# A two-layer decoder trunk on one core: the second half of the residual moved ahead of the second F-chunk's gate products, and the Strassen products of two places moved back by one chunk

## The chip, the cores and the metric

The kernel runs on one core of a Trainium2 chip. The metric is the device time of one execution in microseconds (us); below it is the median of three runs. One more execution was profiled; its trace has, for every instruction, the engine, the line of the kernel, the tiles, the start and the duration. Engines: PE multiplies matrices, DVE and ACT work elementwise (vector and scalar engine), POOL is a third one that is hardly used here, and SP issues most of the loads.

## The reference

The trunk has two layers on 256 tokens of width 2048, all in float32. Each layer is a token mixer (a gated linear recurrence in the first, a gated spatial mixing in the second) and a gated feed-forward block; after each of them the residual is scaled and normalised:

```python
for layer in range(DEPTH):
    mixed = hgrn2_mixer(...) if layer % 2 == 0 else chunked_gmlp(...)
    h = layer_norm(ALPHA * h + mixed, ln1_g[layer], ln1_b[layer])
    ffn = conv_ffn(h, ffn_w_up[layer], ffn_conv_w[layer], ffn_conv_b[layer], ffn_w_down[layer])
    h = layer_norm(ALPHA * h + ffn, ln2_g[layer], ln2_b[layer])

def conv_ffn(x, w_up, conv_w, conv_b, w_down):
    h = x @ w_up                        # (256, 2048) @ (2048, 11264)
    a, b = jnp.split(h, 2, axis=-1)     # 5632 columns each
    a_pad = jnp.pad(a, ((0, 0), (CONV_WIDTH - 1, 0), (0, 0)))
    a = sum(conv_w[j] * a_pad[:, j:j + s_] for j in range(CONV_WIDTH)) + conv_b
    return (jax.nn.silu(a) * b) @ w_down   # (256, 5632) @ (5632, 2048)
```

The change concerns the feed-forward block of both layers.

## The kernel before

**Weights in high and low parts.** A float32 product is made of three products of rounded parts. A weight chunk (512 x 512 floats, 1 MB) is loaded by SP into a buffer `raw`, ACT casts it to the high part `whi` (line 120, two instructions of half a chunk), and DVE subtracts to form the low part `wlo` (line 121, two instructions). `raw`, `whi` and `wlo` have three buffers each, so the cast of a chunk waits until PE has finished the chunk three before it. `chunk` and `seven` take the next prepared chunk and first have all chunks prepared up to three ahead (`AHEAD`, `ahead`).

**Up-products.** `ffn` runs over eleven F-chunks of 512 columns, in groups of 4, 3 and 4. Each F-chunk takes eight up-chunks: four for the convolved branch `a` (the first `block_b` call), then four for the gate branch `b` (the second call). A block ends with its evacuation: ACT copies a part from PSUM (line 381), DVE adds the other (line 382). For `a` DVE then runs the convolution (lines 1095 and 1100) and ACT the silu; for `b` DVE multiplies into `act` (line 1109) and splits the result into `Y` (line 388). PSUM has six banks for blocks (`acc`), each block uses four.

**Down-products.** The hidden state of an F-chunk is multiplied with the down weights and added to the residual `z`. At four places, each made of two neighbouring F-chunks and the first 1024 output columns, the eight block products are replaced by seven (Strassen): `QUADS` names the first F-chunk of the place and, for the seven products in the order `SEVEN`, the position in the order of all up- and down-chunks behind which the product comes. Position 0 is the first up-chunk of the layer; the first F-chunk has 0 to 7, the second 8 to 15 (its gate products are 12 to 15), the third 16 to 23, the fourth 24 to 31, and 32 to 39 are plain down-chunks of the first group. `ffn_order` merges the two lists; `next_up` (after each up-chunk) and the loop of the down-chunks call `sevens`, which runs the products that are due. All four places exist in both layers.

A product is twelve matmuls (`product`, line 215) on the PSUM tiles px. `make` prepares its weights: the first product loads two chunks `b11` and `b12` into the pool `qp`, which stay there; the third and sixth load one more into a `raw` buffer; casts and additions (line 165) follow. `sums` forms four sums of the hidden state (lines 192, 195 and 201), tile `S`, also in `qp`; it is called behind the gate products of the place's second F-chunk.

**The residual.** `residual(c)` scales and shifts 512 columns of `z` with the norm's row vectors, tiles g and b (lines 556 and 557, on DVE, for both halves of the tokens). It is called for c = 0 and 1 behind the gate products of the first F-chunk, for c = 2 and 3 behind those of the second. `issue_after(self.last_lo.ins)` anchors its instructions behind the last low part that the program has asked for by then. `residual(3)` closes the norm's pool; `qp` is opened right after it on the same side of the memory, so the tiles of `qp` overlap those of the norm.

**The order on the engines** is made by a planner at build time: it takes instructions by their order in the program and by its own estimate of when they can run, also on PE, and inserts the semaphores. On the chip each engine follows its list.

Of the kernel before, what the change touches and what calls it, by code (L numbers as in the profile page):

```python
# [19 lines left out]
DFF = 5632  # L20
# [5 lines left out]
NB = 512  # L26
# [5 lines left out]
SUMS = ((0, 1), (0, 3), (1, 2), (2, 1))  # L32
SEVEN = (0, 1, 2, 3, 4, 6, 5)
QUADS = (
# [4 lines left out]
)  # L39
# [12 lines left out]
class Trunk:  # L52
# [1010 lines left out]
    def ffn(self, l, store=None):  # L1063
        nc, tc, a = self.nc, self.tc, self.a
        up, down = a["ffn_w_up"][l], a["ffn_w_down"][l]
        with ExitStack() as st:
            fp = st.enter_context(tc.tile_pool(name=f"fp{l}", bufs=2))
            m = 0
            quads = ExitStack()
            order = self.ffn_order(l)  # L1070
            slots = {}
            self.fresh = {(t, c) for t in range(2) for c in range(4)}

            def sevens():
                while order and order[0][0] == "seven":
                    _, f, which = order.pop(0)
                    self.seven(which, slots[f])

            def next_up(ci):
                assert order.pop(0)[::3] == ("up", ci)  # L1080
                sevens()

            for gi, n in enumerate(FFN_GROUPS):
                acts = []
                for i in range(n):
                    slot = slots[m + i] = FFN_SLOT[gi] + i
                    act = fp.tile([P, 4, S], F32, tag="act", name="act")
                    acts.append(act)

                    def ev_a(j, ps):  # L1090
                        f = 4 * (m + i) + j
                        x = fp.tile([P, S], F32, tag="a", name="a")
                        self.gather(fp, ps, x)
                        cv = act[:, j, :]
                        nc.vector.tensor_scalar(
                            cv, x, self.c(("cw", l, 2), f), self.c(("cb", l), f),
                            ALU.mult, ALU.add,
                        )
                        for d in (1, 2):
                            nc.vector.scalar_tensor_tensor(  # L1100
                                cv[:, d:], x[:, : S - d], self.c(("cw", l, 2 - d), f),
                                cv[:, d:], ALU.mult, ALU.add,
                            )
                        nc.scalar.activation(cv, cv, AF.Silu)

                    def ev_b(j, ps):
                        x = fp.tile([P, S], F32, tag="b", name="b")
                        self.gather(fp, ps, x)
                        nc.vector.tensor_tensor(act[:, j, :], x, act[:, j, :], ALU.mult)
                        self.split(self.Y, 4 * slot + j, act[:, j, :])  # L1110

                    self.block_b(self.X, up, 4, (m + i) * NB, ev_a, halves=m + i == 0,
                                 between=next_up)
                    if m + i == 0:
                        self.xps.close()
                    self.block_b(self.X, up, 4, DFF + (m + i) * NB, ev_b, between=next_up)
                    if m + i in (0, 1):
                        self.residual(2 * i)
                        self.residual(2 * i + 1)
                    if m + i == 1:  # L1120
                        self.qp = quads.enter_context(
                            tc.tile_pool(name=f"qp{l}", bufs=1, side="right")
                        )
                    if (gi, i) in SUMS:
                        self.sums(*acts[-2:])
                end = m + n == NF // CK
                if end:
                    quads.close()
                    st.close()
                    self.norm("ln2", l, store)  # L1130
                    for c in range(4):
                        fs = [x[1] for x in order if x[2] == c]
                        self.block_a(self.Y, slots[fs[0]] * CK, down, fs[0] * CK, len(fs), c * NB,
                                     self.add_z(c, last=True), staggered=c == 3)
                m += n
                while not end and order[0][0] == "down":
                    _, f, c, first, last = order.pop(0)
                    ch = self.chunk(down, f * CK, c * NB)
                    if first:
                        ps = [self.acc.tile([P, NB], F32, tag="acc", name="pa") for _ in range(2)]  # L1140
                    for t in range(2):
                        self.product(ps[t], self.half(slots[f], t), ch, first, last)
                    if last:
                        for t in range(2):
                            self.gain(t, c, ps[t])
                    sevens()
# [59 lines left out]
```

## Time and profile before

| | |
|---|---|
| median of three runs | 2227.26 us (2225.66 to 2228.39) |
| the profiled execution, its time | 2227.53 us |
| its span, first to last instruction | 2225.8 us |
| PE busy | 2198.7 us, 12705 matmuls |
| DVE busy | 1659.9 us |
| ACT busy | 1171.8 us |
| up-weight loads through `raw` | 176 of 1 MB, median 5.0 us to landing |
| loads of `b11` and `b12` | 16 of 1 MB, median 4.9 us to landing |

A row of a timeline has the start in us, the duration in us, the engine and line, the operation, the tiles as output<-inputs, the shapes, and the number of instructions that it merges; in brackets stands how long the engine was idle before it and what ended that. A row of waits has the total of us, the number of waits and the longest. A row of windows has, for each engine, its busy time and its number of instructions, then the granted PE clock (1.00 is full speed), the share of the load engines and GB/s. Matmuls overlap each other, so their durations add to more than the time they take: the pace is seen in the starts. Here and there the record of a matmul is missing, and where it is, the one after it stands in its place.

### The profile page before, as it was taken

The page shows a single profiled execution, that of the slowest core. Times are in us where ns is not written, and L with a number is a line of the kernel's source. Part 1 is how long each engine was busy: PE and PEld are TensorE (multiplying, and loading weights), DVE is VectorE, ACT ScalarE, POOL GpSimd, SP SyncE. Part 2 cuts the span into 40 slices and gives each one's busy share as a digit, 9 for nine tenths or more (in the row PEclk, how much of TensorE's full clock was granted, in tenths as well). Part 3 has the DMA queues.
Part 4 walks back from the last instruction along what each step waited for, and adds up shares of the span by engine and source line. Part 5 has one row for each costly group of instructions (what it writes and reads, how often), then busy time and mean ns, then how long its engine had stood idle before and what let it go on. Part 6 is the DMA issues. An engine that isn't in the chain of part 4 may idle for free.

```text
span 2225.8 us, 31866 instructions
## 1 busy us (share of the span) xinstructions
PE 2198.7 (99%) x12705; PEld 1896.3 (85%) x12705; DVE 1659.9 (75%) x2533; ACT 1171.8 (53%) x1783; POOL 46.8 (2%) x102
## 2 busy tenths in 40 slices
PE   9999999999999999999999999999999999999998
PEld 8888888889788888888888888888788888888886
DVE  6877677668888676877876676567788676877875
ACT  5656575546445454555555545455455454545452
POOL 3000000000000000000000000000000000000000
PEclk9999999999999999999999999999999999999999
DMA  7454645645555665555565665655555656555573
GB/s 269 152 189 143 199 152 170 214 166 188 190 208 189 208 227 190 172 207 189 189 227 187 210 214 192 230 179 172 199 197 190 215 202 207 184 191 174 191 244 114
DMA packets 214597, 430.14 MB, mean 193 GB/s; under 512 B 7577, under 2 KB 9393, under 8 KB 214449
## 3 DMA queue, kind: packets, MB, share of 16 engines
q1 hardware_dynamic: 210080, 415.26, 55.0%
q0 software_dynamic: 4368, 12.85, 1.9%
q8 instruction: 99, 1.62, 0.3%
q14 instruction: 50, 0.40, 0.1%
HBM read 425.98 MB, written 2.10 MB: 192 GB/s over the span
## 4 chain that ended last, share of the span: by engine, by line
PE 92%; DVE 3%; ACT 2%; issue 2%; DMA 1%; POOL 0%; SPq 0%; DVEq 0%; POOLq 0%; ACTq 0%
PE pb L359 36%; PE pb L366 18%; PE pa L215 8%; PE px L215 7%; PE pa L282 6%; PE pa L283 6%; PE pa L281 6%; DVE wlo L121 1%; ACT whi L120 1%; PE pl L796 1%; PE pt L481 1%; DMA b<-in_ffn_w_down_dram 0%; PE pg L1005 0%; DVE z L557 0%; DMA bb<-in_sg_ln_b_dram 0%
## 5 line engine op out<-in xcount | busy, mean ns | idle before, releaser
L359 PE MATMUL pb<-X,whi 128*128 128x512 f32 (+1 forms) x3960 | 1306.1, 384 | 1.9 <-DVE X L495 1.9
L121 DVE TENSOR_TENSOR wlo<-raw,whi 128x1024 fp32r<-128x1024 f32 (+1 forms) x753 | 892.3, 1219 | 450.0 <-ACT whi L120 442.1
L120 ACT CAST whi<-raw 128x1024 fp32r<-128x1024 f32 (+1 forms) x753 | 760.2, 1048 | 697.6 <-PE pb L359 385.9
L366 PE MATMUL pb<-X,wlo 128*128 128x256 f32 x3840 | 1038.0, 278 | 0.0
L359 PEld LDWEIGHTS pb<-X,whi 128*128 128x128 f32 x3960 | 725.7, 188 | 144.0 <-DVE X L495 2.4
L366 PEld LDWEIGHTS pb<-X,wlo 128*128 128x128 f32 x3840 | 713.2, 188 | 7.2 <-DVE wlo L121 0.2
L282 PE MATMUL pa<-wlo,Y 128*128 128x512 f32 x416 | 162.3, 390 | 0.0
L281 PE MATMUL pa<-whi,Y 128*128 128x512 f32 x416 | 162.3, 390 | 0.0
L283 PE MATMUL pa<-whi,Y 128*128 128x512 f32 x416 | 162.0, 389 | 0.0
L215 PE MATMUL pa<-whi,Y 128*128 128x512 f32 x512 | 160.3, 389 | 0.0
L381 ACT COPY rest<-pb 128x256 f32<-128x256 f32 x240 | 87.3, 368 | 97.7 <-PE pb L359 94.7
L215 PEld LDWEIGHTS pa<-whi,Y 128*128 128x128 f32 x512 | 96.1, 188 | 19.7
L121 DVE TENSOR_TENSOR wlo<-b,whi 128x1024 fp32r<-128x1024 f32 x80 | 95.0, 1220 | 14.9 <-ACT whi L120 14.9
L120 ACT CAST whi<-b 128x1024 fp32r<-128x1024 f32 x80 | 80.9, 1050 | 43.0 <-PE pb L359 13.9
L282 PE MATMUL pa<-wlo,X 128*128 128x512 f32 x256 | 99.9, 390 | 0.0
L281 PE MATMUL pa<-whi,X 128*128 128x512 f32 x256 | 99.8, 390 | 0.0
L215 PE MATMUL pa<-wlo,Y 128*128 128x512 f32 x256 | 99.7, 389 | 0.0
L283 PE MATMUL pa<-whi,X 128*128 128x512 f32 x256 | 99.7, 389 | 0.0
L281 PEld LDWEIGHTS pa<-whi,Y 128*128 128x128 f32 x416 | 78.1, 188 | 16.0
L282 PEld LDWEIGHTS pa<-wlo,Y 128*128 128x128 f32 x416 | 78.1, 188 | 16.0
L283 PEld LDWEIGHTS pa<-whi,Y 128*128 128x128 f32 x416 | 78.1, 188 | 15.9
L215 PE MATMUL px<-whi,S 128*128 128x512 f32 x256 | 84.2, 390 | 2.8 <-ACT whi L120 2.8
(191 smaller groups left out, 1816.3 us busy)
## 6 DMA issues: line engine op xcount, KB each, us to landing
raw<-in_ffn_w_up_dram SPq DMA_DIRECT2D x176, 1024.0 KB, 5.0
raw<-in_ffn_w_down_dram SPq DMA_DIRECT2D x72, 1024.0 KB, 4.9
raw<-in_hg_w_in_dram SPq DMA_DIRECT2D x61, 1024.0 KB, 5.0
raw<-in_sg_w_in_dram SPq DMA_DIRECT2D x32, 1024.0 KB, 5.4
raw<-in_hg_w_out_dram SPq DMA_DIRECT2D x16, 1024.0 KB, 4.9
b<-in_ffn_w_down_dram SPq DMA_DIRECT2D x16, 1024.0 KB, 4.9
raw<-in_sg_w_out_dram SPq DMA_DIRECT2D x16, 1024.0 KB, 4.9
g<-in_ln_g_dram POOLq DMA_DIRECT2D x16, 256.0 KB, 5.9
```

The source lines that it names most:

```text
L120: cast = nc.scalar.copy(hi[:, s, :], raw[:, s, :])
L121: self.last_lo = nc.vector.tensor_tensor(lo[:, s, :], raw[:, s, :], hi[:, s, :].bitcast(F32), ALU.subtract)
L215: self.nc.tensor.matmul(ps, x(kk, part), y[:, kk, :], start=start and (kk, part) == (0, 0) and y is hi, stop=stop and (kk, part) == (CK - ...
L281: nc.tensor.matmul(ps[t], xh, hi[:, kk, :], start=n[t] == 0, stop=False)
L282: nc.tensor.matmul(ps[t], xh, lo[:, kk, :], start=False, stop=False)
L283: nc.tensor.matmul(ps[t], xl, hi[:, kk, :], start=False, stop=last)
L359: return self.nc.tensor.matmul(ps[j][:, :, s], ch[0][:, k % CK, c], act[:, k, :, s], start=start and k == 0, stop=k == last, skip_group_ch ...
L366: return self.nc.tensor.matmul(ps[j][:, 1, :], ch[1][:, k % CK, c], act[:, k, 0, :], start=False, stop=False, skip_group_check=loose,)
L381: nc.scalar.copy(r, ps[:, 1, :])
L481: self.last_turn = nc.tensor.transpose(ps[:, j, :], self.z[:, t, k * P : (k + 1) * P], self.ident)
L796: nc.tensor.matmul(ps[n * j : n * j + n, th, :], K[:, own(th, n, j)], moving(th, j), start=True, stop=True, tile_position=(0, n * j),)
```

## The change

Two edits. In `ffn`, the calls `residual(2)` and `residual(3)` and the opening of `qp`, which stood behind the gate products (second `block_b` call) of the second F-chunk, stand ahead of them, behind the products of its convolved branch; the first half of the residual stays where it was. In `QUADS`, all seven products of the first place come one position later (the first behind 18 in place of 17, the last behind 31 in place of 30), and of the second place the first, second, third and fifth.

```diff
 QUADS = (
-    (0, (17, 19, 22, 24, 26, 28, 30)),
-    (2, (32, 34, 37, 40, 42, 45, 47)),
+    (0, (18, 20, 23, 25, 27, 29, 31)),
+    (2, (33, 35, 38, 40, 43, 45, 47)),
     (5, (65, 67, 70, 73, 76, 79, 82)),
     (7, (89, 91, 94, 96, 98, 100, 102)),
 )
...
                     if m + i == 0:
                         self.xps.close()
-                    self.block_b(self.X, up, 4, DFF + (m + i) * NB, ev_b, between=next_up)
-                    if m + i in (0, 1):
-                        self.residual(2 * i)
-                        self.residual(2 * i + 1)
                     if m + i == 1:
+                        self.residual(2)
+                        self.residual(3)
                         self.qp = quads.enter_context(
                             tc.tile_pool(name=f"qp{l}", bufs=1, side="right")
                         )
+                    self.block_b(self.X, up, 4, DFF + (m + i) * NB, ev_b, between=next_up)
+                    if m + i == 0:
+                        self.residual(0)
+                        self.residual(1)
                     if (gi, i) in SUMS:
                         self.sums(*acts[-2:])
```

No instruction is added or removed.

## The prediction

> **What bounds the kernel now.** I read the engine totals first, then the list of waits of the matmul engine (PE), then its timeline where those waits lie, then back along the chain that feeds them.
>
> ```profile
> span 2225.8 us, 31866 instructions
> PE 2198.7 (99%) x12705; PEld 1896.3 (85%) x12705; DVE 1659.9 (75%) x2533; ACT 1171.8 (53%) x1783; POOL 46.8 (2%) x102
> PE px L215 <- ACT whi L120: 7.1, 4, 2.1
> PE px L215 <- DVE wlo L121: 1.5, 2, 0.8
> ```
>
> PE never rests for long, so no work taken off another engine is worth anything unless PE waits for it. The two wait rows are all the waits of the Strassen products (tile px): six, 8.6 us. They lie at the first product of the first place, once per layer:
>
> ```profile
> 602.85 0.39 PE L359 MATMUL pb<-X,whi 128*128 128x512 f32 x1
> 605.37 0.50 PE L215 MATMUL px<-whi,Y 128*128 128x512 f32 x1 [2.13 <-ACT whi L120]
> 606.62 0.50 PE L215 MATMUL px<-wlo,Y 128*128 128x512 f32 x1 [0.76 <-DVE wlo L121]
> ...
> 609.04 0.39 PE L215 MATMUL px<-whi,Y 128*128 128x512 f32 x1
> 611.05 0.50 PE L215 MATMUL px<-whi,S 128*128 128x512 f32 x1 [1.62 <-ACT whi L120]
> 611.39 0.28 PE L366 MATMUL pb<-X,wlo 128*128 128x256 f32 x1
> ...
> 1598.36 0.39 PE L359 MATMUL pb<-X,whi 128*128 128x512 f32 x1
> 1600.88 0.50 PE L215 MATMUL px<-whi,Y 128*128 128x512 f32 x1 [2.14 <-ACT whi L120]
> 1602.14 0.79 PE L215 MATMUL px<-wlo,Y 128*128 128x512 f32 x1 [0.76 <-DVE wlo L121]
> ...
> 1605.92 0.39 PE L215 MATMUL px<-whi,Y 128*128 128x512 f32 x1
> 1607.49 0.50 PE L215 MATMUL px<-whi,S 128*128 128x512 f32 x1 [1.18 <-ACT whi L120]
> ```
>
> The six bracketed waits add to 8.59, the two rows above: the other places have none. The third wait is odd: the matmul at 611.05 belongs to the second product (its operand is S), whose place is two up-chunks later; the planner queued this one matmul early, and the up-chunk stands behind it.
>
> The matmul durations overlap, so the true loss is read from starts. An undisturbed product shows the pace:
>
> ```profile
> 1057.48 0.39 PE L359 MATMUL pb<-X,whi 128*128 128x512 f32 x1
> 1057.70 0.39 PE L215 MATMUL px<-whi,Y 128*128 128x512 f32 x1
> ...
> 1060.42 0.28 PE L366 MATMUL pb<-X,wlo 128*128 128x256 f32 x1
> 1057.00:1125.00 68.00, 68.00 (x381) 59.43 (x380) 58.98 (x77) 36.67 (x50) 0.35 (x1) 1.00 0.53 182
> ```
>
> It starts 0.22 after the matmul before it and lasts 2.72 (1060.42 - 1057.70). Layer 0: the next work was due at 602.85 + 0.22 + 2.72 = 605.79 and began at 611.05: 5.26 lost. Layer 1: due at 1598.36 + 2.94 = 1601.30, began at 1607.49: 6.19 lost. **Together 11.45 us.** Layer 1 loses more because its product ran slowly: from the 1602.14 start to 1605.92 are 3.78 us, in layer 0 from 606.62 to 609.04 only 2.42. The granted clock (the third figure from the right) shows why:
>
> ```profile
> 1602.00:1605.00 3.00, 2.86 (x7) 2.28 (x8) 3.00 (x4) 3.00 (x4) 0.00 (x0) 0.50 0.00 0
> 606.60:609.60 3.00, 2.80 (x11) 1.99 (x11) 3.00 (x3) 3.00 (x4) 0.00 (x0) 1.00 0.03 5
> ```
>
> The same waits halved the clock in one layer and not in the other. [...]
>
> What is late is the load of the first place's weights, as the chain of waits shows:
>
> ```profile
> 598.62 0.70 DVE z L557
> ...
> 599.45 4.79 DMA b<-in_ffn_w_down_dram
> ...
> 604.27 1.05 ACT whi L120
> ...
> 605.34 1.24 DVE wlo L121
> ```
>
> The pool qp takes the memory of the norm's rows g and b, so the load can't begin before the second half of the residual has read them (599.3). Landing, cast and low part follow one after another, and the casts of the next up-chunks stand behind this cast on ACT.
>
> **The change part by part.** *Removed and added:* nothing. All matmuls, DVE operations, casts and loads stay, 16 loads of b in both layers included; only their order differs.
>
> *The residual, earlier.* Eight operations per layer move ahead of the gate products of the second F-chunk. Before:
>
> ```profile
> 593.29 0.68 DVE L556 TENSOR_TENSOR z<-z,g 128x512 f32<-128x512 f32 x1
> ...
> 596.70 1.29 DVE L557 TENSOR_TENSOR z<-z,b 128x512 f32<-128x512 f32 x2
> 597.90 0.69 DVE L556 TENSOR_TENSOR z<-z,g 128x512 f32<-128x512 f32 x1
> 598.62 0.69 DVE L557 TENSOR_TENSOR z<-z,b 128x512 f32<-128x512 f32 x1
> 599.35 0.69 DVE L195 TENSOR_TENSOR s<-act 128x512 f32<-128x512 f32 x1
> ...
> 603.44 1.42 DVE L195 TENSOR_TENSOR S<-s,S 128x512 fp32r<-128x512 f32 x2
> ```
>
> They cost 0.60 each in a pair (596.70 to 597.90 for two), 0.72 where one needs the other (597.90 to 598.62): 4.8 to 5.8. New place, DVE then ACT:
>
> ```profile
> 566.26 2.37 DVE L121 TENSOR_TENSOR wlo<-raw,whi 128x1024 fp32r<-128x1024 f32 x2 [3.12 <-ACT whi L120]
> 568.54 0.75 DVE L382 TENSOR_TENSOR a<-pb,rest 128x256 f32<-128x256 f32 x2
> ...
> 574.32 2.36 DVE L121 TENSOR_TENSOR wlo<-raw,whi 128x1024 fp32r<-128x1024 f32 x2
> ...
> 582.57 2.36 DVE L121 TENSOR_TENSOR wlo<-raw,whi 128x1024 fp32r<-128x1024 f32 x2 [3.08 <-ACT whi L120]
> 588.01 2.36 DVE L121 TENSOR_TENSOR wlo<-raw,whi 128x1024 fp32r<-128x1024 f32 x2 [3.08 <-ACT whi L120]
> 581.49 2.00 ACT L120 CAST whi<-raw 128x1024 fp32r<-128x1024 f32 x2 [3.44 <-PE pb L359]
> ```
>
> They are anchored behind the low part of 566.26 and, in program order, behind the convolution from 568.54. So they end at 574.32 plus 4.8 to 5.8: 579.1 to 580.1. Behind them waits the low part of 574.32. It is that of the third gate chunk, which PE starts at 581.49 (the end of the chunk before it releases the cast of 581.49; chunks are 5.4 apart, as 582.57 and 588.01 are). Its first half needs 1.2 more: 580.3 to 581.3, just in time. I take 0; should one more operation of 1.2 slip in front, about 1 us per layer, so bounds 0 to 2. The next low parts recover in the 3.08 gaps that DVE has at 582 and 588. The loads of the first place can now start at about 580 and land 4.8 later, some 18 us before their use; on SP they pass loads of up-chunks, whose low parts are ready two chunks ahead (588.01 is that of a chunk due at 597.8: 581.49 and three chunks).
>
> With the residual gone from 593 to 599, the sums S (599.35 to 604.86) start right behind the gate's evacuation, about 5 us earlier, and with them all that stands behind them on DVE and ACT.
>
> *The first place, one chunk back.* All seven products move by one up-chunk: 5.4 us more between the evacuation and the first product. Its due time becomes 603.07 + 5.4 = 608.5; even with the old landing its low part would have ended by 607.7 (605.34 + 2.4). So the two edits cover the same wait twice. What moves closer is the rest: the seventh product now stands behind the fourth F-chunk's last gate chunk. Its twin in the last place, which has the old spacing, runs with PE full for 68 us (the 1057 row) and DVE at 58.98 of 68, so there is room. I take 0.
>
> *The second place.* Four of seven move (first, second, third, fifth); the third and fourth come one chunk nearer, to two chunks, as the third and fourth of the first place stand, where none waited. 0.
>
> **Sum:** 2227.53 - 5.26 - 6.19 + 0 = **2216.1 us**, from the profiled execution's own time; the median of the three runs, 2227.26 (2225.66 to 2228.39), lies 0.3 below it.
>
> **Rivals.** *A: the early matmul stays.* The planner may again queue the second product's first matmul right behind the first product. Its cast needs the buffer that this product frees, so the third wait remains, 611.05 - 609.04 less the pace of 0.23 = 1.78, and 1607.49 - 1605.92 - 0.23 = 1.34: 2216.1 + 3.1 = 2219.2. For it: the planner did it in both layers. Against it: it did so with the loads late, and not in the last place. [...]
>
> *B: the residual isn't really earlier.* The anchor sets only the earliest time; the planner may still place it late. Then the sums end at 604.86 as now, the low part of the chunk now ahead of the first product comes behind them, its first half at 606.1, due at 603.2: 2.9 per layer, 2216.1 + 5.8 = 2221.9. Against it: at 593.29 the planner took it as soon as the program had come to it, among the gate's own evacuations. Were A and B both true: 2225.0.
>
> *C: slower, DVE blocked at the sixth product.* Its add waits at the head of DVE's queue for a load, and the fourth F-chunk's evacuation now falls on that stretch:
>
> ```profile
> 668.35 0.39 PE L215 MATMUL px<-whi,S 128*128 128x512 f32 x1
> 663.38 1.22 DVE L165 TENSOR_TENSOR b<-b,raw 128x1024 f32<-128x1024 f32 x1 [2.12 <-DMA raw<-in_ffn_w_down_dram]
> ...
> 674.77 0.75 DVE L382 TENSOR_TENSOR a<-pb,rest 128x256 f32<-128x256 f32 x2
> ```
>
> If DVE keeps this order, the evacuation moves by 5.4 to 680.2. The gate products there begin at 676.5 (668.35, where the fifth product starts before the change, plus the chunk now ahead of it, 5.4, and the product, 2.7) and need the third PSUM bank 0.7 later: 3.0 lost per layer. If the load also lands one load (4.9) later, 7.9: 2216.1 + 15.8 = 2231.9, slower by just 0.2%. It decides against the change from 2.7 us of delay on. Against it: evacuations are earlier in the program than those adds, and DVE idles there.
>
> **How the numbers follow.** Forecast 0.61, its own range 2214.9 (0.3 for the median, and 0.9 of the 1.1 by which the highest run lies above it) to 2218.1 (the third gate chunk late). A 0.13, B 0.11, A and B 0.07, C 0.08. A measurement can tell 0.2%, 4.5 us, from no change. Faster: forecast, A and B, 0.85; within 0.2%: 0.08 (A and B, and part of C); slower 0.07. The range 2214.9 to 2222.4 holds forecast, A and B, 0.85.
>
> **What would show it.** Right: no wait of px in the list of PE's waits; L557 of the second half ending near 580 and the loads of b leaving right after it, in both layers; S operations starting near 594; the clock at 1.00 around the first place. Wrong: a px matmul alone among up-chunks with a wait (A); L557 near 599 (B); PE waits at 676 for a bank (C); a PE wait for the low part near 581 (the bound of 2).

## The result, and the profile after

| | before | after |
|---|---|---|
| median, us (lowest to highest) | 2227.14 (2225.66 to 2228.39), 6 runs | 2213.53 (2212.98 to 2216.72), 6 runs |
| ratio | | 0.9941, 95% interval 0.9928 to 0.9954 |
| the profiled execution | 2227.53 | 2216.72 |

The kernel became 13.6 us faster. The forecast was 2216.1, with a range that began at 2214.9: the direction was right, the gain too small by 2.6, and the time fell below the range. The profiled execution of after is the slowest of its six runs, 3.2 above their median, so its own time looks like the forecast without being evidence for it.

The head of the page of after and the first rows of PE's waits (total us, number, longest):

```profile
span 2215.0 us, 31875 instructions
PE 2196.6 (99%) x12705; PEld 1896.0 (86%) x12705; DVE 1659.3 (75%) x2533; ACT 1170.8 (53%) x1783; POOL 48.8 (2%) x102
PE pb L359 <- DVE X L495: 1.9, 2, 1.1
PE pg L1005 <- DVE y L1010: 1.9, 1, 1.9
```

No row of px is left, the six waits are gone. One row stands out instead: pg, in the spatial gating between the two feed-forward blocks, 1.9 where before had 0.9. PE's timeline around the first place, in both layers:

```profile
606.46 0.39 PE L359 MATMUL pb<-X,whi 128*128 128x512 f32 x1
606.69 0.39 PE L215 MATMUL px<-whi,Y 128*128 128x512 f32 x1
...
609.41 0.28 PE L366 MATMUL pb<-X,wlo 128*128 128x256 f32 x1
...
620.31 0.39 PE L215 MATMUL px<-whi,S 128*128 128x512 f32 x1
...
1599.66 0.39 PE L359 MATMUL pb<-X,whi 128*128 128x512 f32 x1
1599.88 0.39 PE L215 MATMUL px<-whi,Y 128*128 128x512 f32 x1
...
1602.61 0.28 PE L366 MATMUL pb<-X,wlo 128*128 128x256 f32 x1
```

The product now takes 609.41 - 606.69 = 2.72 in layer 0 and 2.73 in layer 1, the pace of the undisturbed one, and the matmul with operand S stands at its own place, at 620.31. The windows over the two products have the granted clock at 1.00 (third figure from the right):

```profile
606.60:609.40 2.80, 2.80 (x14) 2.31 (x13) 2.80 (x3) 2.00 (x2) 0.00 (x0) 1.00 0.00 0
1599.80:1602.60 2.80, 2.80 (x14) 2.30 (x13) 1.67 (x3) 2.00 (x2) 0.00 (x0) 1.00 0.45 110
```

The chain that feeds the place, layer 0, DVE's timeline first, then SP's issues of the two loads:

```profile
572.50 1.28 DVE L556 TENSOR_TENSOR z<-z,g 128x512 f32<-128x512 f32 x2
...
576.11 1.29 DVE L557 TENSOR_TENSOR z<-z,b 128x512 f32<-128x512 f32 x2
577.31 6.90 DVE L121 TENSOR_TENSOR wlo<-raw,whi 128x1024 fp32r<-128x1024 f32 x6
587.95 2.36 DVE L121 TENSOR_TENSOR wlo<-raw,whi 128x1024 fp32r<-128x1024 f32 x2 [3.74 <-ACT whi L120]
...
595.51 0.68 DVE L195 TENSOR_TENSOR s<-act 128x512 f32<-128x512 f32 x1
...
599.18 1.22 DVE L121 TENSOR_TENSOR wlo<-b,whi 128x1024 fp32r<-128x1024 f32 x1
```

```profile
577.87 0.37 SPq L154 DMA_DIRECT2D b<-in_ffn_w_down_dram  x1
...
582.39 1.42 SPq L154 DMA_DIRECT2D b<-in_ffn_w_down_dram  x1
```

The residual ends at 577.40 instead of 599.3, the first load leaves right behind it and the second at 582.39, and the low part that the product waited for is made from 599.18 on, 7.5 before its use at 606.69.

**Where the 13.6 us come from** is seen by cutting both executions at the same five matmuls: the first product of the first mixer (pd), the last of that mixer (L926), the first of the spatial gating (pg), the last transposes ahead of layer 1's block (pt) and the last Strassen product (px). PE's timeline of before, then of after:

```profile
79.34 0.46 PE L796 MATMUL pd<-q,k 128*32 128x32 f32 x32
...
500.25 0.39 PE L926 MATMUL pa<-whi,Y 128*128 128x512 f32 x1
...
1332.84 0.49 PE L1005 MATMUL pg<-wsT,v 128*128 128x128 f32 x3
...
1506.49 0.60 PE L481 MATMUL pt<-ident,z 128*128 128x128 f32 x4
...
2144.09 0.39 PE L215 MATMUL px<-whi,Y 128*128 128x512 f32 x1
```

```profile
76.99 0.46 PE L796 MATMUL pd<-q,k 128*32 128x32 f32 x32
...
497.89 0.39 PE L926 MATMUL pa<-whi,Y 128*128 128x512 f32 x1
...
1325.65 0.49 PE L1005 MATMUL pg<-wsT,v 128*128 128x128 f32 x3
...
1502.38 0.60 PE L481 MATMUL pt<-ident,z 128*128 128x128 f32 x4
...
2133.31 0.39 PE L215 MATMUL px<-whi,Y 128*128 128x512 f32 x1
```

Differences of neighbouring rows: layer 0 went from 832.59 to 827.76, 4.83 saved; layer 1 from 637.60 to 630.93, 6.67 saved; **together 11.50, where the sum said 11.45.** The agreement to 0.05 is partly luck: layer 0 saved 0.43 less than its 5.26, layer 1 0.48 more than its 6.19. And the start, which the change doesn't touch, was 2.35 shorter, and the spatial gating, also untouched, 3.08 longer (173.65 to 176.73). The rest of the difference has to be looked for in more executions.

### The profile page after: what moved, and what is told of

The parts are those of the page before. It is cut to its first block, busy times and chain, and to the rows that moved or that the text cites. A ratio compares the mean times of both kernels' runs of the same rounds, so it can differ in the third digit from the quotient of the medians.

```text
span 2215.0 us, 31875 instructions
## 1 busy us (share of the span) xinstructions
PE 2196.6 (99%) x12705; PEld 1896.0 (86%) x12705; DVE 1659.3 (75%) x2533; ACT 1170.8 (53%) x1783; POOL 48.8 (2%) x102
## 3 DMA queue, kind: packets, MB, share of 16 engines
q8 instruction: 99, 1.62, 0.3%
## 4 chain that ended last, share of the span: by engine, by line
PE 93%; DVE 2%; ACT 2%; issue 1%; DMA 1%; POOL 0%; SPq 0%; DVEq 0%; POOLq 0%; ACTq 0%
PE pb L359 37%; PE pb L366 19%; PE pa L215 8%; PE px L215 7%; PE pa L283 6%; PE pa L282 6%; PE pa L281 6%; DVE wlo L121 1%; ACT whi L120 1%; PE pl L796 1%; PE pt L481 0%; DMA bb<-in_sg_ln_b_dram 0%; PE pg L1005 0%; PE pa L928 0%; PE pa L926 0%
```

## The experiments

Four questions. Is the gain of the two layers a constant, or one draw of something that varies (theory: the six waits are always there, but the clock's answer to them isn't)? Are the start and the gating the change's doing? Does each edit alone take the wait away, as the prediction said? And how much room is at the new place of the residual? The table holds, of every profiled execution, the stages cut as above, in us (without the first mixer, 421 to 422, and the end, 81.7); the last two columns are where the granted clock was 0.5 before the end of the program, and the median.

| kernel | start | layer 0 | gating | layer 1 | half clock at (for us) | median |
|---|---|---|---|---|---|---|
| before | 79.3 | 832.6 | 173.7 | 637.6 | 7.7 (3.4), 1601.7 (3.4) | 2227.14 |
| before, second | 79.4 | 833.4 | 173.6 | 637.5 | 9.1 (3.4), 1603.2 (3.4) | 2228.59 |
| before, third | 77.7 | 835.9 | 172.6 | 636.7 | 604.2 (10.2) | 2227.17 |
| before, fourth | 77.1 | 834.6 | 173.0 | 636.4 | 606.7 (3.4) | 2226.05 |
| after | 77.0 | 827.8 | 176.7 | 630.9 | 1330.1 (3.4) | 2213.53 |
| after, second | 77.0 | 827.8 | 172.7 | 630.9 | none | 2213.90 |
| residual alone | 77.3 | 827.8 | 177.0 | 630.9 | 1330.7 (3.4) | 2215.17 |
| places alone | 77.3 | 828.6 | 172.9 | 631.8 | none | 2215.70 |
| before, residual delayed | 77.1 | 835.6 | 173.4 | 640.6 | 604.6 (6.8), 1604.7 (6.8) | 2231.61 |
| after, residual delayed | 76.7 | 831.0 | 172.6 | 633.6 | none | 2219.11 |
| after, old second place | 77.3 | 827.2 | 173.6 | 630.9 | none | 2214.71 |
| after, gating's residual early | 76.7 | 827.3 | 172.5 | 630.8 | none | 2213.97 |

### The kernel before, three more times

No edit.

> The kernel before, unchanged, for a second profile of it. Of the 13.6 us between the medians the two places explain 11.5 to 12.0 by the first pair of profiles; that pair also differs at the start (the after one is 2.4 us quicker up to the first products) and at the spatial gating (the after one waits 1.86 in place of 0.93 and has a half-clock window there, 3.1 us in all). Theory 'chance': start and half-clock windows fall differently from execution to execution, so this profile differs from the first one in at least one of them (start within 0 to 2.4 us of it, half-clock windows at the places in 0, 1 or 2 layers), and the loss at the two places lies between 10.5 and 13.3. Rival 'fixed': start, windows and the loss of 11.45 come out as in the first profile, and the rest of the gain belongs to the change. Time by both: ratio 1.000, within 0.001.

> The kernel before once more, for a third profile. So far a half-clock window followed where PE stood for 1.86 us or more within one of the 3.41 us windows, and none where it stood for 1.76 or less. Theory 'start by chance': the landing of the second piece of x, 7.4 and 8.0 us in the two profiles of this kernel and 6.7 to 7.0 in four others, scatters by itself; here it may come at 7.0 or below, then the first mixing product starts near 77.0 and not 79.35. Rival 'start belongs to this kernel': again 7.4 or later, half clock right behind it, first mixing product at 79.3 to 79.4.

> As the third profile of the kernel before: by chance, the first mixing product starts at 77.0 to 79.4; by the rival, at 79.3 to 79.4 for the fourth time. At the two places the loss is 4.8 to 6.7 us per layer, the upper end where a half-clock window follows.

The second time the kernel gave 2228.59 beside 2227.98 for the same program in the same group, ratio 1.000 [0.9991, 1.0009]; the third and fourth are single times. The second profile repeats the long start, as the rival theory has it, the third and fourth don't. All eight first products have their wait of 2.13 to 2.28 and the 0.76 behind it; what follows differs. PE's timeline of the third, layer 0, and the window over the half clock:

```profile
603.77 0.50 PE L215 MATMUL px<-whi,Y 128*128 128x512 f32 x1 [2.20 <-ACT whi L120]
605.03 0.80 PE L215 MATMUL px<-wlo,Y 128*128 128x512 f32 x1 [0.76 <-DVE wlo L121]
...
611.27 0.79 PE L215 MATMUL px<-whi,S 128*128 128x512 f32 x1 [1.18 <-ACT whi L120]
```

```profile
604.20:614.40 10.20, 8.26 (x21) 6.15 (x21) 10.20 (x10) 6.26 (x7) 0.00 (x0) 0.50 0.31 100
```

The first two waits are those of the first execution, but here the clock stays at half speed for 10.2 us, three times 3.4. Against after's 827.8 and 630.9 the two layers lose 11.5, 12.2, 13.9 and 12.3 (832.6 + 637.6 - 1458.7 and so on), mean 12.5; a stretch of slower pace, the subject of the last section, moves these by up to 0.5. Sorted by the clock: layers at full speed lose 4.8 to 5.8, those with one half-speed stretch of 3.4 us 6.6 to 6.8, the one with three 8.1. In each of the four executions exactly one layer was hit.

Which layer is hit can be read from the traces. The two half-speed stretches of the first execution last 3.41 us each (7.70 to 11.11 and 1601.73 to 1605.14) and begin 1594.02 us apart, 467 times 3.4133. From the end of the second to the half speed at the end of the program, at 2219.54, are 614.40, 180 times 3.4133; in the first profile of after, from 1333.55 to 2207.37, 873.82, 256 times. Counted on in these steps, the program falls into windows of 3.41 us. The two windows of that execution that hold most of the first wait, layer 0 and then layer 1:

```profile
601.63:605.04 3.41, 1.60 (x10) 1.14 (x8) 3.16 (x5) 2.01 (x3) 0.00 (x0) 1.00 1.05 408
1598.32:1601.73 3.41, 0.93 (x4) 0.30 (x2) 2.89 (x4) 3.16 (x5) 0.00 (x0) 1.00 1.01 390
```

PE (the first busy time) stood still for 3.41 - 1.60 = 1.81 in the one, because the wait ran on into the next window, and for 2.48 in the other. Half speed followed the second alone. The same count over all twelve profiles leaves no exception: each of the ten windows at full clock with 1.86 us or more of idle PE was followed by half speed, and so were the twelve at the ends of the programs, where PE has finished; none of the windows with 1.82 or less was. A half-speed window with 0.54 or more of idle PE was followed by another one (4 of 4), one with 0.51 or less by full speed (10 of 10): in the third execution the three windows held 0.76, 0.89 and 0.29. So the same wait halves the clock or not, as it falls on these windows. The kernel doesn't set them: in the four executions of before, half speed first begins 0.9, 2.3, 0.0 and 2.5 us behind a whole number of steps from the first instruction.

The start varies too: 79.3, 79.4, 77.7, 77.1. PE's timeline at the second piece of x, in before and then in after:

```profile
7.56 0.95 PE L481 MATMUL pt<-ident,z 128*128 128x128 f32 x4 [1.99 <-DMA z<-in_x_dram]
```

```profile
7.12 0.63 PE L481 MATMUL pt<-ident,z 128*128 128x128 f32 x4 [0.84 <-DMA z<-in_x_dram]
```

The matmuls of before last 0.95 for four, of after 0.63: behind the wait of 1.99 the clock fell to half. The second execution of before is alike (1.91, half clock from 9.1); the two others waited less than 1 us and have no half-speed stretch there.

### The changed kernel once more

No edit.

> The changed kernel, unchanged, for a second profile. Theory 'chance': the half-clock window at the spatial gating is absent or elsewhere, the start is between that of the two first profiles, the profiled execution takes about 2213.5, and no px wait appears. Rival 'fixed': again 2216.7 in the profiled execution with the window at 1330. Time by both: ratio 0.994.

2213.90 (2212.98 to 2214.21), ratio 0.9934 [0.9921, 0.9946]. The two layers are the same to 0.1 us as in the first profile of after, and the gating is back at 172.7: the 3.1 us more differ between executions of one program. They came again with the residual alone (177.0). The row of the gating in the first profile of after, and the window behind it:

```profile
1328.80 1.16 PE L1005 MATMUL pg<-wsT,v 128*128 128x128 f32 x8 [1.86 <-DVE y L1010]
```

```profile
1330.10:1333.50 3.40, 3.40 (x12) 2.92 (x12) 3.40 (x9) 2.49 (x7) 0.15 (x1) 0.51 0.67 252
```

A stall of 1.86, then 3.4 us at half speed. PE waits there for DVE, and DVE had waited 2.3 for the norm's rows gb in this stretch, in the second profile 0.9. Why the rows come later in some executions stays open.

### Each edit alone

The residual alone (places as before):

```diff
-    (0, (18, 20, 23, 25, 27, 29, 31)),
-    (2, (33, 35, 38, 40, 43, 45, 47)),
+    (0, (17, 19, 22, 24, 26, 28, 30)),
+    (2, (32, 34, 37, 40, 42, 45, 47)),
```

> Only the residual and the opening of the pool are moved; both places stand as before. Theory 'the edits cover the same wait twice': the load leaves near 578, the first product finds its weights ready at its old place (due about 601 on the new clock), no early matmul of the second product, at most 0.5 us per layer lost at the chunk after it: 2213.5 to 2214.5, ratio 0.994. Rival 'the place has to move': casts and low parts behind the first product are still late as in the kernel before, 1.5 to 3 us per layer: 2216.5 to 2219.5, ratio 0.9955 to 0.997.

The places alone (the calls of the residual as before):

```diff
+                    self.block_b(self.X, up, 4, DFF + (m + i) * NB, ev_b, between=next_up)
+                    if m + i in (0, 1):
+                        self.residual(2 * i)
+                        self.residual(2 * i + 1)
                     if m + i == 1:
-                        self.residual(2)
-                        self.residual(3)
                         self.qp = quads.enter_context(...)
-                    self.block_b(self.X, up, 4, DFF + (m + i) * NB, ev_b, between=next_up)
```

> Only the places are moved; the residual stays behind the gate products. The load still leaves near 599 and lands near 604; the first product is due at 608.5. Theory 'the edits cover the same wait twice': its low part ends by 607.7, no wait there; the additions and the next low part end just in time (first half 611.2 against 611.3), 0 to 1 us per layer: 2213.5 to 2215.5, ratio 0.994 to 0.995. Rival B of the prediction: what stands behind the late sums is late, 2.9 us per layer: 2219, ratio 0.9965.

2215.17 (2213.62 to 2218.72), ratio 0.9938 [0.9924, 0.9951], and 2215.70 (2214.69 to 2217.24), ratio 0.9943 [0.9931, 0.9956]: **either edit alone brings nearly the whole gain.** The medians lie 0.7 and 0.2 above what the theory 'the edits cover the same wait twice' forecast, and below what the rivals did. In neither is there a wait of px. The rows of PE's timeline that are left, in the kernel with the residual alone and then with the places alone:

```profile
605.57 0.38 PE L366 MATMUL pb<-X,wlo 128*128 128x256 f32 x1 [0.34 <-DVE wlo L121]
```

```profile
607.82 0.39 PE L215 MATMUL px<-whi,Y 128*128 128x512 f32 x1
...
611.63 0.38 PE L366 MATMUL pb<-X,wlo 128*128 128x256 f32 x1 [0.46 <-DVE wlo L121]
...
1601.84 0.39 PE L366 MATMUL pb<-X,wlo 128*128 128x256 f32 x1 [0.47 <-DVE wlo L121]
```

With the places alone the loads still leave late, from SP:

```profile
598.64 0.92 SPq L154 DMA_DIRECT2D b<-in_ffn_w_down_dram  x2
```

Yet the product, one chunk later, finds its weights ready. What stays is some 0.8 us per layer: the chunk behind the product waits for its low part, which stands on DVE behind the additions for the second product. That 1.7 (828.6 - 827.8 and 631.8 - 630.9) agrees with 2215.70 - 2213.90 = 1.8: this small remainder is what the residual adds once the places are moved. With the residual alone the two layers are as short as with both edits, so the places add nothing there that the layers show; the median is 1.3 above, and the intervals overlap.

### A delay ahead of the residual, in both kernels

Eight DVE passes per layer that multiply `z` by 1 and add 0, ahead of the second half of the residual:

```diff
                 zz = self.z[:, t, c * NB : (c + 1) * NB]
+                for _ in range(2 if c > 1 and self.slow else 0):
+                    nc.vector.tensor_scalar(zz, zz, 1.0, 0.0, ALU.mult, ALU.add)
```

> The kernel before with eight passes over z that multiply by 1 and add 0, ahead of the second half of the residual where it stood (about 0.55 us each, 4.4 per layer). Theory 'the load waits for the residual and PE for the load': load, cast and first product come 4.4 later in both layers, 8.8 in all, and PE stands for a whole window, so a half-clock window follows in both layers, 1 us more in each: 2237 to 2240, ratio 1.004 to 1.0055. Rival 'something else holds the first product': time as before, ratio 1.000 to 1.001.

> The changed kernel with the same eight passes ahead of the second half of the residual at its new place. Theory 'the new place is just covered': the low part of the third gate chunk, ready 1.1 us ahead of its use, comes 3.3 us late, PE waits for it in both layers, perhaps with a half-clock window behind it: 2220 to 2223, ratio 0.997 to 0.998 against the kernel before. Rival 'there is much room at the new place': as the changed kernel, 2213.5 to 2215, ratio 0.994.

The delay came out smaller than the expectations reckon; their 0.55 per pass was the author's estimate, and the `TENSOR_SCALAR` of line 546 in before (z<-z,mv, the same shape) has a mean duration of 0.543. DVE's timeline of the delayed changed kernel:

```profile
576.00 1.43 DVE L558 TENSOR_SCALAR z<-z 128x512 f32<-128x512 f32 x4
577.34 1.29 DVE L559 TENSOR_TENSOR z<-z,g 128x512 f32<-128x512 f32 x2
578.54 1.29 DVE L560 TENSOR_TENSOR z<-z,b 128x512 f32<-128x512 f32 x2
579.75 6.90 DVE L122 TENSOR_TENSOR wlo<-raw,whi 128x1024 fp32r<-128x1024 f32 x6
```

Four passes take 577.34 - 576.00 = 1.34, so one costs 0.34 and eight 2.7; the two-tensor operations beside them cost 0.60. Why an operation with one tensor as operand costs 0.34 here and one with two 0.60, no run shows.

*In the kernel before* the delay gave 2231.61 (2230.37 to 2232.98) against 2227.64, ratio 1.0016 [1.0007, 1.0026], between the two forecasts. The waits decide for the theory 'the load waits for the residual'. Its chain of waits, then PE's timeline:

```profile
599.02 0.70 DVE z L560
599.84 4.98 DMA b<-in_ffn_w_down_dram
604.84 1.05 ACT whi L121
```

```profile
605.94 0.79 PE L216 MATMUL px<-whi,Y 128*128 128x512 f32 x1 [4.99 <-ACT whi L121]
```

The first wait grew from 2.13 to 2.28 up to 4.99 (4.87 in layer 1), by the delay: the chain residual, load, cast, product is the one that sets the time. The time rose by 4.0 and not by 2 x 2.7; the third wait is gone, since here the planner queues no matmul of the second product early.

*In the changed kernel* the delay gave 2219.11 (2218.22 to 2220.16), 5.2 above the changed kernel of another group, ratio to before 0.9958 [0.9942, 0.9975]: just below the forecast of the theory 'just covered', whose delay was taken too long. PE's timeline:

```profile
580.51 0.74 PE L360 MATMUL pb<-X,whi 128*128 128x512 f32 x2 [1.14 <-ACT whi L121]
...
593.38 0.50 PE L360 MATMUL pb<-X,whi 128*128 128x512 f32 x1 [0.96 <-DVE b L383]
...
1573.26 0.74 PE L360 MATMUL pb<-X,whi 128*128 128x512 f32 x2 [1.14 <-ACT whi L121]
```

No px waits. A wait comes up at the third gate chunk, the place that the prediction named. DVE's low part of that chunk began at 579.75, 2.44 later than in after, where it was 0.9 ahead; the 1.5 that remain are near the wait of 1.14. But the profile puts the first matmul down to a cast of ACT instead, one of high weights that the planner here set ahead of the low ones; why it waits for that cast was not followed, and the low part, ready at 579.75 + 1.2 = 581.0, would have been the next limit. In layer 0 there is a second wait at 593.38, for a PSUM bank: the later loads of b held up a load of an up-chunk on SP (b at 580.30, up-chunks from 582.13 on, in after 577.87 and 579.69), its cast came at 589.54 (586.87 in after), and DVE reached the evacuation behind its low part late. Of layer 1's 2.7 only about 1.4 lie in the wait; the rest is a slower pace of the matmuls ahead of the place (below).

### The second place, and the residual of the gating layer

The second place alone back at its old positions, and, in another kernel, the residual ahead of the spatial gating called one chunk earlier:

```diff
-    (2, (33, 35, 38, 40, 43, 45, 47)),
+    (2, (32, 34, 37, 40, 42, 45, 47)),
```

```diff
-                if c in (1, 2):
-                    self.residual(2 * c - 2)
-                    self.residual(2 * c - 1)
+                if c in (0, 1):
+                    self.residual(2 * c)
+                    self.residual(2 * c + 1)
```

> The changed kernel with the second place at its old positions (32, 34, 37, 40, 42, 45, 47); the first place and the residual stay moved. Theory 'the second place is worth nothing': no wait of PE at either place, 2213 to 2215, ratio 0.9935 to 0.9945, as the changed kernel. Rival 'the two places have to move together': the seventh product of the first place now stands one chunk ahead of the first of the second, whose cast and additions come late by up to a chunk's share, 1 to 3 us per layer: 2216 to 2220, ratio 0.995 to 0.997.

> The changed kernel with the same kind of move in the spatial gating: the four residual calls there come behind the first and second column block in place of the second and third. PE waits there for 0 to 2.2 us for y (six of ten profiles under 1 us), and where it stood 1.86 or more a half-clock window followed, 3.1 us in all. Theory 'the loads there wait for the residual': rows gb and bb leave some 22 us earlier, no wait, no window: 2212.5 to 2214, the ratio 0.0005 below that of the changed kernel at most, hardly to be told. Rival 'they wait for their own buffers': the third and fourth loads leave behind the first use of v as before, the wait stays between 0 and 2.2: 2213 to 2216.5.

2214.71 (2213.70 to 2217.87), ratio 0.9942 [0.9930, 0.9955]; and 2213.97 (2212.78 to 2214.64), ratio 0.9938 [0.9925, 0.9952]. Neither differs measurably from the changed kernel's 2213.53 and 2213.90. With the old second place all other products of layer 0 stand at the same distances from each other as in after, to 0.03 us: those positions are worth nothing. The earlier residual of the gating doesn't beat the changed kernel; its one profile has no wait of pg, but neither has the second of after.

## Why the prediction was wrong, point by point

**The place and the mechanism: right.** The wait came from the load behind the second half of the residual (it grew with the delay), it was gone after, and the two layers gained 11.50 in the pair of profiles, 11.45 forecast, with errors of 0.4 and 0.5 that offset each other. "The two edits cover the same wait twice" is shown by the two kernels with one edit each. *Second place 0*: right.

**The failed step is the term "5.26 + 6.19" of the sum, taken as a constant, and with it the low end of the range.** The term is one execution's draw, and it stops counting too early. Against after the two layers of before lost 11.5 to 13.9 over four executions, mean 12.5, because half-speed stretches follow the waits or not, and can follow each other. The prediction saw that the same waits halved the clock in one layer and not in the other, but the sum takes the one pair of losses that it read. Reckoned as in the prediction, from starts up to the early matmul of S, the four executions lose 11.5, 11.5, 12.5 and 11.8, mean 11.8. The rest lies behind that matmul: in the third execution half speed lasts until 614.4, 3.1 us beyond it; in layer 1 of the first, PE ran the up-chunk behind it (from 1607.83 on) in pairs 0.35 apart and not 0.34. **Left out altogether was the start:** that of the profiled execution was 79.34, that of the four 78.4 on average, that of the two profiles of after 77.0. The 2227.53 that the sum starts from holds the long one, and is also 0.4 above the median of 2227.14. With 11.45 and no start in the sum the forecast was 2.6 too high, and a low end only 1.2 below it, made of the spread of three runs, couldn't hold that.

How the 13.6 between the medians splits is not shown, since the median runs have no trace. In the profiles the layers give 12.5 on average and the start 1.4, but in the two of after the first mixer is 0.3 and the gating 1.5 longer, so that the whole spans differ by 12.0, and by 13.2 with the second of after alone.

Why the start is longer in some executions stays open: two of before's four have it, none of the eight profiles of the other kernels. The order doesn't explain it, for up to the first product of the mixer the matmuls, DVE, ACT, POOL and SP run the same operations in the same order in before and after. Yet a start of 79.3 with the shortest other stages of after's two profiles would take 2215.0, and ten of after's eleven times lie at 2214.21 or below, the eleventh being the first profile, which has the short start. That speaks against equal chances in both kernels.

**The residual's new time: right, with an offset.** 579.1 to 580.1 was forecast, 577.40 measured; 2.35 of the difference is the shorter start. The third gate chunk, which PE began at 579.46, had the first half of its low part at 577.31 + 1.2 = 578.5: 0.9 ahead, "just in time", and its price 0. With 2.7 more of DVE ahead of it, PE waits at this chunk.

**The loads on SP: placed rightly, their effect missed.** They pass loads of up-chunks, as said, but the room of two chunks was taken for enough. The low part that began at 588.01 before, after 3.08 of idling, begins at 587.95 after 3.74, on a clock that runs 2.35 ahead: 2.3 later. So the sums S start at 595.51, which is 1.5 earlier than before's 599.35 when the start is taken off, not 5. It cost nothing here, since 7.5 of room is left ahead of the product; with the delay on top it became the wait at 593.38.

**Rival A** didn't come: the planner put no matmul of S early. Its price was wrong as well. DVE's timeline of before at the third wait:

```profile
609.89 3.49 DVE L121 TENSOR_TENSOR wlo<-raw,whi 128x1024 fp32r<-128x1024 f32 x3
```

The up-chunk behind the early matmul needs the first of these three low parts, done at about 611.1; the early matmul started at 611.05. Without it PE would have waited about as long there for DVE, so in layer 0 the early matmul cost next to nothing. In layer 1, where the product ran at half speed, the same low part began at 1605.41 and was done at about 1606.6, the early matmul started at 1607.49: there it cost some 0.9. The prediction put the third wait of both layers, 3.1, down to the early matmul alone. **Rival B**: L557 ends at 577.40, so no. **Rival C**: no wait of PE near 676, and PE's list has none for a bank.

**The clock.** That the same waits halved the clock in one layer and not in the other was read rightly. In the twelve profiles the granted clock in such a stretch is 0.5 (0.51 in the one at 1330.1 in after), a stretch lasts 3.4 us or two or three times that, and the steps go on through the program (1594.02 us are 467 of them). A whole step of idle PE isn't needed: the ten windows inside the programs that brought half speed held 1.86 to 3.41 us of idle PE, and only one of them was wholly idle. That it depends on where a stall falls is what the windows of 1.81 and 2.48 show.

## What to carry to other kernels

In these profiles a stall of PE could cost more than its length, by an amount that differs between executions of one program (in layer 0 waits of 2.13, 0.76 and 1.62 went with a loss of 4.8 in the first, of 2.20, 0.76 and 1.18 with 8.1 in the third): before a sum goes into a forecast, several executions are cut at the same matmuls, and the stages that the edit doesn't touch give the uncertainty of those that it does. A stall of some 2 us halved the clock there 8 of 12 times, by where it fell on windows that the kernel doesn't set. Where two edits cover one wait, the second is worth what the first leaves over, here 0.8 us per layer at most. A buffer that is freed earlier starts its transfer earlier (here at 577.87, before at 599.45), and that transfer then stood ahead of others on its queue: a low part on DVE came 2.3 us later for it, and the evacuation behind it, and only the room of 7.5 ahead of the product hid that.

## What the runs showed of the hardware beside this

**Half the clock after a short stall.** In the twelve profiles PE stood still for 1.86 us or longer 14 times, and 10 times the granted clock went to 0.5 within 4 us, for 3.4, 6.8 or 10.2 us. None of the shorter stalls (1.62 and less) began such a stretch. Of twelve stalls of 1.86 to 2.28 four stayed at full speed; in all four the wait was split between two of the windows counted above, and neither window held more than 1.82 us of idle PE. What decides in these profiles is thus the idle time of PE summed within one window of 3.41 us, with a limit between 1.82 and 1.86. No run moved a wait by intent against the windows, so nothing beyond these twelve profiles is shown.

**Two paces of the same matmuls at full clock.** In the delayed changed kernel a stretch ahead of the place in layer 1 ran slower than in after; the windows of the one and of the other, first the kernel with the delay:

```profile
1517.00:1528.00 11.00, 11.00 (x64) 9.63 (x63) 8.41 (x19) 5.41 (x9) 0.00 (x0) 1.00 0.54 197
```

```profile
1519.50:1530.50 11.00, 11.00 (x66) 9.70 (x66) 7.34 (x16) 6.04 (x10) 0.00 (x0) 1.00 0.55 190
```

64 against 66 matmuls in 11.00 us, both at 1.00 and with PE full. The starts show pairs 0.350 apart in place of 0.340, over tens of us. In after's layer 0 such a stretch lies ahead of the place: 606.46 - 497.89 = 108.57, less one chunk of 5.44, is 103.13, where before has 602.85 - 500.25 = 102.60. It made layer 0's gain 0.5 smaller. The stretch comes and goes between executions: the second and the fourth of before have it ahead of the place as well (103.2 and 103.1). Its cause stays open.
